# A decoder step on one core: norm weight folded into the weights' splits, set-up beside the norm, written engine order

## The chip, the core and the metric

The kernel runs on one core of one Trainium2 chip. The metric is the device time of one execution in microseconds. The kernel before took 2430.19 us (median of 3 runs, 2428.37 to 2430.72).

## The reference

One layer of a decoder trunk for 2048 prompt tokens and 8 x 4 sample tokens (2080 columns in all), float32, width 1024:

```
[u_pool | u_ssm | gates] = RMSNorm(x) * norm_mix @ w_in        # 1024 -> 512 + 512 + 2048
a     = PoolMixer(u_pool)                                      # windows of 2, 4, 8, 16 tokens
y     = S5(u_ssm)            # 32 groups, a complex diagonal scan over tokens, state 64 per group
merged = sigmoid(g0) * (a @ w_branch_pool) + sigmoid(g1) * (GLU(gelu(y)) @ w_branch_ssm)
h     = x + merged @ w_out
h     = h + SwiGLU(RMSNorm(h));   output = RMSNorm(h), and the last states of pooling and S5
```

S5 first turns its parameters into powers of a complex number: exponentials, a sine and a cosine, products (`_s5_discretise` and what follows from it).

## The kernel before, in words

Every float32 matmul is done as three float16 matmuls (`mm3`): a matrix is scaled by a power of two and split into a high half (ScalarE, ACT: `hi` = x times scale) and a low half (VectorE, DVE: `lo` = x times scale minus `hi`).

**Norm and the SSM columns** (`norm_in`). Tokens come in 16 blocks of 128 rows and one of 32. For each, ACT squares and sums (`sq`, L220), DVE makes the reciprocal root (`rstd_of`), GpSimd (POOL) multiplies the block by the norm weight (`xgp`, L230; the first two blocks on DVE, L123), the block is split (L52, L53), TensorE (PE) transposes it (L135) and ACT and DVE copy the two halves out of PSUM into `xh` and `xl` (L136). Beside that, `proj` multiplies column slices of 256 tokens with chunks 2 and 3 of `w_in`, the SSM columns; a slice has four column tiles, and ACT takes each out of PSUM (`uo`, L248), SyncE (SP) stores it to `u_d` in DRAM (L250). `w_in` is prepared by chunks of 256 columns (`Win.prep`): a sum of squares on ACT (L89), the maximum over partitions (by PE for the first chunks, by POOL for the others), a power of two by small operations on DVE (L99 to L101, L44 to L47), one split of the whole chunk.

**S5** (`S5`). `setup` loads the parameters (L391 to L422, on SP), transposes `an` and computes on DVE, about 150 operations, most of them 48 columns wide. `run` goes over four units of eight groups: matrices (`vmat`, `tmat`), states (L570), a scan on DVE (L582, L584), outputs (L643, L644). Every `yield n` of it lets `put` emit n column tiles of the other ten chunks of `w_in` (`chunk`, 100 tiles of 24 matmuls); `Win.prep` of the chunk after next stands at the start of each chunk. Then pooling, branches, output projection and the feed-forward part follow, with the remaining tiles beside the first of them.

**Order.** A planner puts each engine's instructions in order by priority (order in the program) and by what it believes to be ready. Inside `tc.manual_schedule(engines=IN_ORDER)` PE, DVE, ACT and POOL keep the written order; SP stays with the planner. Before, only the feed-forward part has it (L919). `ps` holds PSUM tiles: tag "mm" 4 banks for column tiles, "s5" 2 and "tp" 2.

Of the kernel before, what the change touches and what calls it, by code (L numbers as in the profile page):

```python
# [24 lines left out]
D = 1024  # L25
# [59 lines left out]
def pow2_root(E, x, junk, ps=None):  # L85
# [32 lines left out]
def norm_parts(E, wk, x, w, r, g, s):  # L118

    nc = E.nc  # L120
# [18 lines left out]
class Win:  # L139


    def __init__(self, E, ctx, w_in, inv_x):
        self.E, self.w, self.inv_x = E, w_in, inv_x
# [11 lines left out]
    def prep(self, c, ps=None, half=None):  # L155
# [9 lines left out]
        nc.vector.tensor_tensor(cc[:, 0:1], inv, self.inv_x, op=OP.mult)  # L165
        nc.vector.tensor_scalar(cc[:, 1:2], cc[:, 0:1], 0.5, None, op0=OP.mult)
# [13 lines left out]
def norm_in(E, ps, win, x_p, x_s, norm_mix, xh, xl, u_d):  # L180

    nc, tc = E.nc, E.tc
    with ExitStack() as ctx:
        ld = ctx.enter_context(tc.tile_pool(name="xld", bufs=7))
# [14 lines left out]
        g = bcast_row(E, wk, norm_mix, D, "gmix", bufs=1)  # L199
# [5 lines left out]
        gm = E.const.tile([128, 2], F32, name="gmx")  # L205
        nc.vector.tensor_reduce(gm[:, 0:1], g, axis=AX.X, op=OP.max, apply_absolute_value=True)
        nc.vector.tensor_scalar(gm[:, 1:2], gm[:, 0:1], 32.001, None, op0=OP.mult)
        s, inv = pow2(E, gm[:, 1:2])
        nc.vector.tensor_copy(E.inv_x, inv)
        sx = E.const.tile([128, 1], F32, name="sx")  # L210
        nc.vector.tensor_copy(sx, s)

        def norm(bs):

            w = BLK[bs[0]][1]
            steps = []
            ss = E.small.tile([128, len(bs)], F32, tag=f"ss{len(bs)}", name="ss")
            for i, b in enumerate(bs):
                sq = wk.tile([128, D], BF16, name="sq", bufs=1)
                nc.scalar.activation(sq[:w], X[b][:w], AF.Square, accum_out=ss[:w, i:i + 1])  # L220
            r = rstd_of(E, ss[:w], len(bs), w)
            rs = E.small.tile([128, len(bs)], F32, tag=f"rx{len(bs)}", name="rx")
            nc.vector.tensor_scalar(rs[:w], r, sx[:w], None, op0=OP.mult)
            for i, b in enumerate(bs):
                x = X.pop(b)
# [18 lines left out]
        def proj(n0, w, cs=((2, 0), (2, 1), (3, 0), (3, 1)), steps=()):  # L244
            for j, (c, cb) in enumerate(cs):
                q, cc = win.mm(ps, c, cb, xh, xl, n0, w)
                o = wk.tile([128, 512], F32, name="uo", bufs=3)
                nc.scalar.activation(o[:, :w], q[:, :w], AF.Copy, scale=cc[:, 0:1])  # L248
                r0 = (c - 2) * 256 + cb * 128
                nc.sync.dma_start(u_d[r0:r0 + 128, n0:n0 + w], o[:, :w])  # L250
                for f in steps[j::len(cs)]:
                    f()

        win.prep(2, ps, 0)
        for f in norm([0]):
            f()
        win.prep(2, ps, 1)
        for f in norm([1]):
            f()
        loads_to(4)  # L260
        T = {1: norm([2, 3])}
        proj(0, 128, ((2, 0), (2, 1)))
        win.prep(3, ps)
        proj(128, 128, ((2, 0), (2, 1)))
        loads_to(6)
        for p in range(7):
            if p < 6:
                T[p + 2] = norm([2 * p + 4, 2 * p + 5])
                loads_to(2 * p + 9)
            else:  # L270
                T[7] += norm([16])
            if p == 3:
                win.load(0)
            proj(p * 256, 256, ((2, 0), (2, 1), (3, 0), (3, 1))[0 if p else 2:], T.pop(p + 1))
        win.load(1)
        proj(1792, 288)
        win.prep(0)

# [19 lines left out]
NG = 32  # L298
# [11 lines left out]
def exp_f32(E, pool, x, n, tag):  # L310
# [8 lines left out]
    nc.vector.scalar_tensor_tensor(r, k, 2.12194440e-4, r, op0=OP.mult, op1=OP.add)  # L319
    nc.vector.tensor_scalar(p, r, 1.0 / 5040, None, op0=OP.mult)  # L320
    for c in (1.0 / 720, 1.0 / 120, 1.0 / 24, 1.0 / 6, 0.5, 1.0):
        nc.vector.scalar_tensor_tensor(p, p, c, r, op0=OP.add, op1=OP.mult)
    nc.vector.tensor_scalar(e.bitcast(I32), k, 127.0, 8388608.0, op0=OP.add, op1=OP.mult)
# [4 lines left out]
def sincos_f32(E, pool, x, n):  # L328
# [9 lines left out]
    tt(E, z, r, r, OP.mult)  # L338
    nc.vector.tensor_scalar(s, z, -1.9515295891e-4, 8.3321608736e-3, op0=OP.mult, op1=OP.add)
    tt(E, s, s, z, OP.mult)  # L340
    nc.vector.scalar_tensor_tensor(s, s, -1.6666654611e-1, z, op0=OP.add, op1=OP.mult)
    nc.vector.scalar_tensor_tensor(s, s, 1.0, r, op0=OP.add, op1=OP.mult)
    nc.vector.tensor_scalar(c, z, 2.443315711809948e-5, -1.388731625493765e-3, op0=OP.mult, op1=OP.add)
# [3 lines left out]
    nc.vector.tensor_scalar(c, c, 1.0, None, op0=OP.add)  # L347
    out = pool.tile([128, 2, n], F32, name="sco")
    for i, (f, o) in enumerate(((s, c), (c, s))):
# [10 lines left out]
        tt(E, out[:, i], a, sg, OP.mult)  # L360
    return out[:, 0], out[:, 1]


class S5:
# [5 lines left out]
    def setup(self):  # L370
        E, nc, w, ps = self.E, self.E.nc, self.w, self.ps
# [16 lines left out]
        with E.tc.tile_pool(name="s5s", bufs=1, side="right", reuse_waits="tile") as s:  # L388
            ld = s.tile([128, n], F32, name="ldt")
            dt = w["ssm_log_dt"]  # L390
            nc.sync.dma_start(ld[:, :NG], bass.AP(tensor=dt.tensor, offset=dt.offset, ap=[[0, 128], [1, NG]]))  # L391
            for h in range(2):
                nc.sync.dma_start(ld[h * 64:h * 64 + 64, NG:],
                                    bass.AP(tensor=dt.tensor, offset=dt.offset + h, ap=[[0, 64], [2, NG // 2]]))
            an = s.tile([NG, 2, 3, 128], F32, name="an")
            ap = ps.tile([128, 512], F32, name="mm", tag="s5", bufs=2)
            for i, nm in enumerate(("ssm_a_re", "ssm_a_im")):
                a = w[nm]
                src = a.rearrange("o g p -> (o g) p")
                nc.sync.dma_start(an[:, i, 0, 0:64], src)  # L400
                nc.sync.dma_start(an[:, i, 0, 64:128], src)
                nc.sync.dma_start(an[:16, i, 1], bass.AP(tensor=a.tensor, offset=a.offset, ap=[[128, 16], [1, 128]]))
# [4 lines left out]
            BA = s.tile([128, NG, HD], F32, name="ba")  # L407
            BB = s.tile([128, NG, HD], F32, name="bb")
            for h, (x, y) in enumerate((("ssm_b_re", "ssm_b_im"), ("ssm_b_im", "ssm_b_re"))):
                nc.sync.dma_start(BA[h * 64:h * 64 + 64], w[x].rearrange("o g p h -> p (o g) h"))  # L410
                nc.sync.dma_start(BB[h * 64:h * 64 + 64], w[y].rearrange("o g p h -> p (o g) h"))
            cn = s.tile([128, 4, 2, 128], F32, name="cn")
            for i, nm in enumerate(("ssm_c_re", "ssm_c_im")):
                src = w[nm].rearrange("o g h p -> (o g h) p").rearrange("(t r) p -> r t p", r=128)
                nc.sync.dma_start(cn[:, :, 0, i * 64:i * 64 + 64], src)
                nc.sync.dma_start(cn[:, :, 1, (1 - i) * 64:(1 - i) * 64 + 64], src)
            sn = s.tile([128, 2, 128], F32, name="sn")
            for i, nm in enumerate(("state_ssm_re", "state_ssm_im")):
                src = w[nm].rearrange("o b g p -> (o b g) p").rearrange("(t r) p -> r t p", r=128)
                nc.sync.dma_start(sn[:, :, i * 64:i * 64 + 64], src)  # L420
            nc.vector.memset(dv[96:128], 0.0)
# [1290 lines left out]
```

## Time and profile before

| | before |
|---|---|
| median of 3 runs | 2430.19 us |
| profiled execution | 2434.37 us |
| its span, first to last instruction | 2432.2 us |
| PE busy | 2298.3 us (94%) |
| DVE busy | 1641.4 us (67%) |
| ACT busy | 1021.6 us (42%) |
| POOL busy | 425.8 us (18%) |

The durations below are those of the profiled execution. In the page's slices a digit is the busy share in tenths of one fortieth of the span, 60.8 us; PEclk is the clock granted to TensorE, where 1.00 is 2.4 GHz and 0.50 is 1.2 GHz. A wait is idle time of an engine, put down to what ended it last.

### The profile page before, as it was taken

To read this page: it belongs to the slowest core of one execution; us is meant where nothing else is said; L and a number is where in the kernel's file an instruction comes from. 1 tells how busy PE (TensorE), PEld (TensorE's weight loads), DVE (VectorE), ACT (ScalarE), POOL (GpSimd) and SP (SyncE) were. 2 spreads that over 40 slices of the span, in tenths; PEclk is the share of its full clock that TensorE was granted. 3 is DMA by queue.
4 is the path that set the end of the run, shared out by engine and by line. 5 is a ranking of instruction groups with operands and counts; after the bars stand their busy time and mean duration, and the time that the engine had idled before them with its cause. 6 is when DMAs were issued, how large, how long until landed. Compare 5 with 4: busy or idle time off the path is not lost. (4 is left out here: it accounts for less than half of the span.)

```text
span 2432.2 us, 43171 instructions
## 1 busy us (share of the span) xinstructions
PE 2298.3 (94%) x16939; PEld 1613.6 (66%) x16939; DVE 1641.4 (67%) x3866; ACT 1021.6 (42%) x1808; POOL 425.8 (18%) x443
## 2 busy tenths in 40 slices
PE   5869999999999999997999999999999999989998
PEld 4745566565578875554888888888888864433543
DVE  7516784757658778777555554655555688789887
ACT  7421333323445442445444454544544552243332
POOL 2300000000000000000111221211112345355342
PEclk9889999999999999998999999999999999999999
DMA  6215133335434334413221222222212344444332
GB/s 215 72 49 124 54 90 91 102 90 198 141 118 126 114 109 159 156 64 115 70 88 53 79 76 65 79 62 79 79 53 79 126 141 142 151 169 141 122 124 78
DMA packets 209776, 258.02 MB, mean 106 GB/s; under 512 B 33046, under 2 KB 170582, under 8 KB 209053
## 3 DMA queue, kind: packets, MB, share of 16 engines
q1 hardware_dynamic: 209397, 254.83, 33.7%
q8 instruction: 132, 2.16, 0.4%
q14 instruction: 71, 0.58, 0.1%
q10 hardware_dynamic: 144, 0.26, 0.0%
q0 software_dynamic: 32, 0.18, 0.0%
HBM read 167.56 MB, written 86.67 MB: 105 GB/s over the span
## 5 line engine op out<-in xcount | busy, mean ns | idle before, releaser
L851 PEld LDWEIGHTS <-W 128*128 128x128 f16 x7392 | 726.3, 98 | 114.0 <-issue 13.9
L851 PE MATMUL p<-m,W 128*128 128x256 f16 (+1 forms) x3084 | 356.6, 275 | 1.4 <-ACT v L883 1.4
L114 PE MATMUL mm<-xl,wh 128*128 128x512 f16 (+4 forms) x1072 | 347.4, 325 | 8.0 <-DVE xl L136 8.0
L113 PE MATMUL mm<-xh,wh 128*128 128x512 f16 (+4 forms) x1072 | 347.9, 326 | 1.5 <-ACT xh L136 1.4
L115 PE MATMUL mm<-xh,wl 128*128 128x512 f16 (+4 forms) x1072 | 347.2, 325 | 1.6 <-DVE wl L53 1.6
L113 PE MATMUL pd<-m,W 128*128 128x512 f16 x616 | 236.4, 384 | 17.8 <-DVE xr L1098 7.7
L115 PE MATMUL pd<-m,W 128*128 128x512 f16 x616 | 236.3, 384 | 0.4 <-DVE W L307 0.4
L114 PE MATMUL pd<-m,W 128*128 128x512 f16 x616 | 236.6, 384 | 0.0
L851 PE MATMUL p<-x,W 128*128 128x256 f16 x1848 | 207.3, 274 | 2.9 <-ACT p L872 2.8
L851 PE MATMUL p<-xq,W 128*128 128x256 f16 x1764 | 198.4, 274 | 4.8 <-ACT p L872 3.5
L884 POOL TENSOR_TENSOR p<-v,p 128x256 f32<-128x256 f32 (+1 forms) x88 | 72.0, 818 | 666.1 <-ACT v L883 523.3
L115 PEld LDWEIGHTS <-wl 128*128 128x128 f16 x1072 | 107.1, 100 | 76.7 <-issue 9.8
L307 DVE TENSOR_TENSOR w<-u,p 128x272 f32<-128x272 f32 (+1 forms) x86 | 36.5, 425 | 172.8 <-PE p L851 169.2
L114 PEld LDWEIGHTS <-wh 128*128 128x128 f16 x1072 | 106.9, 100 | 67.5 <-issue 2.5
L113 PEld LDWEIGHTS <-wh 128*128 128x128 f16 x1072 | 106.8, 100 | 64.6 <-issue 0.3
L1097 POOL TENSOR_TENSOR xq<-xq,xr 128x512 f32<-128x512 f32 x90 | 128.8, 1451 | 42.0 <-DVE xq L1098 17.3
L114 PEld LDWEIGHTS <-W 128*128 128x128 f16 x616 | 60.9, 99 | 92.9 <-issue 23.3
L115 PEld LDWEIGHTS <-W 128*128 128x128 f16 x616 | 60.9, 99 | 75.4 <-issue 3.5
L113 PEld LDWEIGHTS <-W 128*128 128x128 f16 x616 | 60.9, 99 | 74.4 <-issue 3.4
L292 ACT ACTIVATE go<-mm,wc 128x512 f32<-128x512 f32 (+1 forms) x80 | 47.6, 603 | 139.9 <-PE mm L115 113.6
L883 ACT COPY v<-p 128x272 f32<-128x272 f32 (+1 forms) x86 | 32.2, 375 | 165.1 <-PE p L851 162.7
L113 PE MATMUL po<-woh,m 128*128 128x512 f16 x256 | 97.0, 379 | 0.9 <-DVE x L307 0.9
(472 smaller groups left out, 4429.2 us busy)
## 6 DMA issues: line engine op xcount, KB each, us to landing
f_d<-m SPq DMA_DIRECT2D x44, 512.0 KB, 3.1
xq<-f_d SPq DMA_DIRECT2D x40, 512.0 KB, 4.7
x<-in_x_prompt_dram SPq DMA_DIRECT2D x32, 512.0 KB, 4.7
xq<-h_d SPq DMA_DIRECT2D x32, 512.0 KB, 4.1
g<-g_d SPq DMA_DIRECT2D x56, 256.0 KB, 2.7
g_d<-go SPq DMA_DIRECT2D x48, 256.0 KB, 2.7
gr<-in_ffn_w_gate_dram SPq DMA_DIRECT2D x23, 512.0 KB, 4.3
ur<-in_ffn_w_up_dram SPq DMA_DIRECT2D x23, 512.0 KB, 4.9
```

Of the source, the lines that this page charges most:

```text
L113: nc.tensor.matmul(q, ah, bh, start=first, stop=False)
L114: nc.tensor.matmul(q, ah, bl, start=False, stop=False)
L115: nc.tensor.matmul(q, al, bh, start=False, stop=last)
L292: nc.scalar.activation(o[:, :w], q[:, :w], AF.Tanh, scale=cc[:, 1:2])
L307: E.nc.vector.tensor_tensor(o, a, b, op=op)
L851: nc.tensor.matmul(q, W[:, x, a, ka], X[b][:, y, k, :w], start=begin and k == v == 0, stop=end and k == 3 and v == 2, skip_group_check=True)
L883: nc.scalar.copy(v, x)
L884: nc.gpsimd.tensor_tensor(p5, v, p5, op=OP.add)
L1097: add = (lambda o, x: tt(E, o, o, x, OP.add)) if end else (lambda o, x: nc.gpsimd.tensor_tensor(o, o, x, op=OP.add))
```

## The change

The norm weight no longer multiplies the tokens; it multiplies the rows of `w_in`. The half chunks of the first chunk (2) are multiplied on DVE before their preparation; for every other chunk the split is done in eight pieces of 256 columns, each with a scale per partition that contains the weight, and the bound from the sum of squares is multiplied by the largest weight squared. POOL's product is gone. The SSM column stores are issued by ACT. S5's loads are emitted in slice 1 of the norm, and its set-up, now a generator, goes on by two pieces after each column tile from slice 3 on. Norm and S5 part stand in written order, and chunk 0 is prepared at the norm's end. The outputs of S5 are preceded by 3, 3, 5, 6 column tiles in the four units (before 10, 4, 3, 3).

```diff
-def pow2_root(E, x, junk, ps=None):
+def pow2_root(E, x, junk, ps=None, f=None):
     nc.scalar.activation(junk, x, AF.Square, accum_out=m[:, 0:1])
+    if f is not None:
+        nc.vector.tensor_tensor(m[:, 0:1], m[:, 0:1], f, op=OP.mult)
...
+SX = 512.0
-def norm_parts(E, wk, x, w, r, g, s):
-    if g is not None:
-        xg = wk.tile([128, D], F32, name="xg", tag="xg", bufs=1)
-        nc.vector.scalar_tensor_tensor(xg[:w], x[:w], r, g[:w], op0=OP.mult, op1=OP.mult)
-        x, r = xg, s[:w]
+def norm_parts(E, wk, x, w, r):
...
-    def __init__(self, E, ctx, w_in, inv_x):
+    def __init__(self, E, ctx, w_in, g):
+        self.g = E.const.tile([128, KB], F32, name="gmix")
+        E.nc.scalar.dma_start(self.g, g.rearrange("o (k p) -> p (o k)", p=128))
+        self.g2 = E.const.tile([128, 2], F32, name="gmx2")
+        E.nc.vector.tensor_reduce(self.g2[:, 0:1], self.g, axis=AX.X, op=OP.max, apply_absolute_value=True)
+        E.nc.vector.tensor_tensor(self.g2[:, 1:2], self.g2[:, 0:1], self.g2[:, 0:1], op=OP.mult)
...
-        s, inv = pow2_root(E, t[:, :, n], wh[:, :, n].bitcast(BF16), ps)
-        split(E, wh[:, :, n], wl[:, :, n], t[:, :, n], s)
+        if half is not None:
+            nc.vector.tensor_tensor(t[:, :, n], t[:, :, n],
+                                    self.g[:, :, None].to_broadcast([128, KB, n.stop - n.start]), op=OP.mult)
+        s, inv = pow2_root(E, t[:, :, n], wh[:, :, n].bitcast(BF16), ps, self.g2[:, 1:2] if half is None else None)
+        if half is not None:
+            split(E, wh[:, :, n], wl[:, :, n], t[:, :, n], s)
+        else:
+            gs = E.small.tile([128, KB], F32, tag="gs", name="gs")
+            nc.vector.tensor_scalar(gs, self.g, s, None, op0=OP.mult)
+            for k in range(KB):
+                split(E, wh[:, k], wl[:, k], t[:, k], gs[:, k:k + 1])
...
-        ld = ctx.enter_context(tc.tile_pool(name="xld", bufs=7))
+        ld = ctx.enter_context(tc.tile_pool(name="xld", bufs=6))
...
-                if b < 2:
-                    hi, lo = norm_parts(E, wk, x, w, r[:, i:i + 1], g, sx)
-                else:
-                    xg = wk.tile([128, D], F32, name="xgp", bufs=2)
-                    nc.gpsimd.tensor_tensor(xg[:w], x[:w], g[:w], op=OP.mult)
-                    hi, lo = norm_parts(E, wk, xg, w, rs[:w, i:i + 1], None, None)
+                hi, lo = norm_parts(E, wk, X.pop(b), w, rs[:w, i:i + 1])
...
+        def cols(n0, w, c, cb):
+            q, cc = win.mm(ps, c, cb, xh, xl, n0, w)
+            o = wk.tile([128, 288], F32, name="uo", bufs=4)
+            nc.scalar.activation(o[:, :w], q[:, :w], AF.Copy, scale=cc[:, 0:1])
+            r0 = (c - 2) * 256 + cb * 128
+            nc.scalar.dma_start(u_d[r0:r0 + 128, n0:n0 + w], o[:, :w])
+
+        setup = s5.setup()
+        g = norm([0])
+        step(g, 2)
         win.prep(2, ps, 0)
+        step(g)
+        put(0)
+        g = norm([1])
+        step(g, 2)
         win.prep(2, ps, 1)
+        step(g)
+        loads_to(5)
+        cols(0, 128, 2, 0)
+        put(1)
+        g = norm([2, 3])
+        step(g, 2)
+        cols(0, 128, 2, 1)
+        step(g, 2)
         win.prep(3, ps)
+        cols(128, 128, 2, 0)
+        cols(128, 128, 2, 1)
+        put(2)
+        put(3)
+        for p in range(8):
+            bs = [2 * p + 4, 2 * p + 5] if p < 6 else [16] if p == 6 else []
+            nb = [b for b in (2 * p + 2, 2 * p + 3) if p and b < 16] + ([16] if p == 7 else [])
+            g = norm(bs) if bs else iter(())
+            loads_to(2 * p + 9)
+            if p == 1:
+                s5.loads()
             if p == 3:
                 win.load(0)
+            if p == 6:
+                win.load(1)
+            f = [f for b in nb for f in T.pop(b)] if p else []
+            cc = ((2, 0), (2, 1), (3, 0), (3, 1))
+            n0, w = (p * 256, 256)
+            if p == 7:
+                for x in f:
+                    x()
+                w = 288
+            step(g)
+            for j, (c, cb) in enumerate(cc):
+                if p == 0 and j < 2:
+                    step(g)
+                    continue
+                cols(n0, w, c, cb)
+                if p < 7:
+                    for x in (f[:1], f[1:3], f[3:], ())[j]:
+                        x()
+                step(g)
+                if p > 2:
+                    step(setup, 2)
+            step(g, 4)
         win.prep(0)
+        for _ in setup:
+            pass
...
-        yield (10, 4, 3, 3)[un]
+        yield (3, 3, 5, 6)[un]
...
-        norm_in(E, ps, win, w["x_prompt"], w["x_sample"], w["norm_mix"], xh, xl, u_d)
         with ExitStack() as cs:
             s5 = S5(E, cs, ps, w, u_d, y_d, [(outs[3], outs[6]), (outs[4], outs[7])])
-            s5.setup()
+            with E.tc.manual_schedule(engines=IN_ORDER):
+                norm_in(E, ps, win, w["x_prompt"], w["x_sample"], xh, xl, u_d, s5)
+            s5.pools()
...
-            for n in s5.run():
-                put(1 if n is None else n)
+            with E.tc.manual_schedule(engines=IN_ORDER):
+                for n in s5.run():
+                    put(1 if n is None else n)
```

In the new `norm_in`, `norm(bs)` is a generator (squares; reciprocal root; one split per block), `put(b)` transposes a block and copies it out, `step(g, n)` takes n pieces of a generator. `S5.loads` holds the set-up's tiles and DMAs, `S5.setup` its 27 pieces of arithmetic with the same operations as before.

## Rows read from the trace of the kernel before

**Rows 1.** The page's slices, busy tenths in 40 slices of 60.8 us.

```profile
PE   5869999999999999997999999999999999989998
...
PEclk9889999999999999998999999999999999999999
```

**Rows 2.** Busy time by stretch: length, engines' busy us, PEclk, DMA share, GB/s.

```profile
60.00:100.00 40.00, 29.96 (x264) 25.41 (x265) 28.07 (x51) 20.83 (x29) 20.35 (x9) 0.83 0.29 93
100.00:160.00 60.00, 59.70 (x540) 47.74 (x538) 16.76 (x32) 25.20 (x33) 6.30 (x9) 1.00 0.19 61
160.00:182.00 22.00, 1.35 (x6) 0.48 (x5) 0.79 (x5) 0.69 (x1) 0.00 (x0) 0.60 0.12 9
182.00:240.00 58.00, 54.52 (x290) 30.84 (x289) 38.79 (x169) 10.07 (x15) 1.31 (x2) 0.91 0.55 126
240.00:300.00 60.00, 54.16 (x276) 32.30 (x275) 47.70 (x201) 19.93 (x37) 2.68 (x2) 0.91 0.14 48
300.00:400.00 100.00, 99.71 (x553) 60.35 (x552) 63.57 (x231) 32.23 (x64) 2.47 (x9) 1.00 0.40 95
```

**Rows 3.** PE's waits, 0 to 160 us: total, times, longest us.

```profile
PE tp L135 <- ACT hi L52: 9.2, 3, 4.6
```

**Rows 4.** ACT's groups, 0 to 160 us: count, busy us, mean ns, idle.

```profile
L220 ACT ACTIVATE sq<-x 128x1024 bf16<-128x1024 f32 x16 | 16.8, 1052 | 2.7 <-DMA x<-in_x_prompt_dram 2.6
L136 ACT COPY xh<-tp 128x1024 f16<-128x1024 f16 x16 | 16.0, 1010 | 3.6 <-PE tp L135 3.5
L52 ACT ACTIVATE hi<-xgp,rx 128x1024 f16<-128x1024 f32 x14 | 16.0, 1147 | 9.3 <-POOL xgp L230 9.3
L248 ACT ACTIVATE uo<-mm,wc 128x256 f32<-128x256 f32 x26 | 12.2, 470 | 33.1 <-PE mm L115 28.2 <-ACT hi L52 3.0 <-issue 1.8
```

**Rows 5.** PE's waits, 160 to 640 us.

```profile
PE mm L403 <- DMA an<-in_ssm_a_re_dram: 20.7, 1, 20.7
```

**Rows 6.** SP's queue, 157 to 189 us: start, us, instruction, count.

```profile
157.47 1.46 SPq L393 DMA_DIRECT2D ldt<-in_ssm_log_dt_dram  x2
...
171.57 0.60 SPq L410 DMA_DIRECT2D ba<-in_ssm_b_re_dram  x1
...
187.68 0.47 SPq L420 DMA_DIRECT2D sn<-in_state_ssm_im_dram  x1
```

**Rows 7.** DVE's groups by shape, 0 to 160 us.

```profile
L53 DVE SCALAR_TENSOR_TENSOR lo<-xgp,rx,hi 128x1024 f16<-128x1024 f32 x14 | 23.9, 1719 | 4.5 <-ACT hi L52 4.3
L136 DVE COPY xl<-tp 128x1024 f16<-128x1024 f16 x16 | 10.9, 687 | 36.8 <-PE tp L135 36.7
...
L53 DVE SCALAR_TENSOR_TENSOR wl<-wr,pw,wh 128x1024 f16<-128x1024 f32 x2 | 2.6, 1280 | 0.0
```

**Rows 8.** One source line: ACT's only DMA issue, ns min/median/max.

```profile
L1137 ACTq DMA_DIRECT2D out_dram<-xq x1: 374/374/374, 2429.3 to 2429.3; - x1
```

**Rows 9.** DVE in order of time, a chain of set-up.

```profile
182.48 1.43 DVE L322 SCALAR_TENSOR_TENSOR exa<-exa 128x48 f32<-128x48 f32 x6
```

**Rows 10.** Busy time in set-up and in one scan.

```profile
186.00:210.00 24.00, 22.20 (x130) 12.74 (x129) 23.43 (x135) 3.17 (x6) 0.00 (x0) 1.00 0.45 129
479.00:511.00 32.00, 32.00 (x172) 16.65 (x171) 32.00 (x161) 6.62 (x10) 0.35 (x1) 1.00 0.14 52
```

**Rows 11.** ACT in order of time, preparation of chunk 0.

```profile
144.06 1.91 ACT L89 ACTIVATE wh<-wr 128x2048 bf16<-128x2048 f32 x1 [2.14 <-PE mm L114]
145.88 0.19 ACT L89 ACTIVATION_READ_ACCUMULATOR wh<-wr 128x1 f32 x1
...
148.00 2.00 ACT L52 ACTIVATE wh<-wr,pw 128x2048 f16<-128x2048 f32 x1 [0.45 <-DVE wc L165]
```

**Rows 12.** ACT's groups by shape, 182 to 705 us.

```profile
L292 ACT ACTIVATE go<-mm,wc 128x512 f32<-128x512 f32 x48 | 32.6, 682 | 100.3 <-PE mm L115 82.6 <-issue 17.6
...
L519 ACT COPY v<-mm 128x512 f32<-128x512 f32 x8 | 4.4, 587 | 13.8 <-PE mm L518 13.8
...
L52 ACT ACTIVATE bh<-bt,bk 128x256 f16<-128x256 f32 x4 | 2.0, 508 | 2.0 <-DVE bt L1403 2.0
```

More of the change, by code (lines that the diff above doesn't have):

```diff
@@ L242, in loads_to, with put @@
                 nl[0] += 1
[L244 to L252, printed above, removed]
+        def put(b):
+            for f in T.pop(b):
+                f()
@@ new lines, in step @@
+        def step(g, n=1):
+            for _ in range(n):
+                next(g, None)
+        def cols(n0, w, c, cb):
[7 more added lines that the diff above has]
+        step(g, 2)
@@ L368, in __init__, with loads @@
         self.E, self.ctx, self.ps, self.w, self.u_d, self.y_d, self.outs = E, ctx, ps, w, u_d, y_d, outs
-    def setup(self):
-        E, nc, w, ps = self.E, self.E.nc, self.w, self.ps
+    def loads(self):
+        E, nc, w = self.E, self.E.nc, self.w
         K = self.ctx.enter_context(E.tc.tile_pool(name="s5k", bufs=1, side="right", reuse_waits="tile"))
@@ L387, in setup @@
         self.ymx = K.tile([128, 4], F32, name="ymx")
[L388 to L395, printed above, removed]
-            ap = ps.tile([128, 512], F32, name="mm", tag="s5", bufs=2)
[L397 to L402, printed above, removed]
+        self.lx = ExitStack()
@@ new lines, in loads @@
+        s = self.lx.enter_context(E.tc.tile_pool(name="s5l", bufs=1, side="right", reuse_waits="tile"))
+        ld = s.tile([128, n], F32, name="ldt")
+        dt = w["ssm_log_dt"]
+        nc.sync.dma_start(ld[:, :NG], bass.AP(tensor=dt.tensor, offset=dt.offset, ap=[[0, 128], [1, NG]]))
+        for h in range(2):
+            nc.sync.dma_start(ld[h * 64:h * 64 + 64, NG:],
+                              bass.AP(tensor=dt.tensor, offset=dt.offset + h, ap=[[0, 64], [2, NG // 2]]))
+        an = s.tile([NG, 2, 3, 128], F32, name="an")
@@ new lines, in loads @@
+        for i, nm in enumerate(("ssm_a_re", "ssm_a_im")):
+            a = w[nm]
+            src = a.rearrange("o g p -> (o g) p")
+            nc.sync.dma_start(an[:, i, 0, 0:64], src)
+            nc.sync.dma_start(an[:, i, 0, 64:128], src)
+            nc.sync.dma_start(an[:16, i, 1], bass.AP(tensor=a.tensor, offset=a.offset, ap=[[128, 16], [1, 128]]))
+        BA = s.tile([128, NG, HD], F32, name="ba")
+        BB = s.tile([128, NG, HD], F32, name="bb")
+        for h, (x, y) in enumerate((("ssm_b_re", "ssm_b_im"), ("ssm_b_im", "ssm_b_re"))):
+            nc.sync.dma_start(BA[h * 64:h * 64 + 64], w[x].rearrange("o g p h -> p (o g) h"))
+            nc.sync.dma_start(BB[h * 64:h * 64 + 64], w[y].rearrange("o g p h -> p (o g) h"))
@@ new lines, in loads @@
+        cn = s.tile([128, 4, 2, 128], F32, name="cn")
+        for i, nm in enumerate(("ssm_c_re", "ssm_c_im")):
+            src = w[nm].rearrange("o g h p -> (o g h) p").rearrange("(t r) p -> r t p", r=128)
+            nc.sync.dma_start(cn[:, :, 0, i * 64:i * 64 + 64], src)
+            nc.sync.dma_start(cn[:, :, 1, (1 - i) * 64:(1 - i) * 64 + 64], src)
+        sn = s.tile([128, 2, 128], F32, name="sn")
+        for i, nm in enumerate(("state_ssm_re", "state_ssm_im")):
+            src = w[nm].rearrange("o b g p -> (o b g) p").rearrange("(t r) p -> r t p", r=128)
+            nc.sync.dma_start(sn[:, :, i * 64:i * 64 + 64], src)
@@ new lines, in loads, with setup @@
+        nc.vector.memset(dv[96:128], 0.0)
+        nc.sync.dma_start(dv[112:128], w["ssm_d"].rearrange("o (g h) -> h (o g)", h=HD))
+        self.L = ld, an, BA, BB, cn, sn
+    def setup(self):
+        E, nc, w, ps = self.E, self.E.nc, self.w, self.ps
+        n = NG + NG // 2
+        P, EL, S0, S0P, BT, CT, PV = self.P, self.EL, self.S0, self.S0P, self.BT, self.CT, self.PV
+        ld, an, BA, BB, cn, sn = self.L
+        with self.lx, E.tc.tile_pool(name="s5s", bufs=1, side="right", reuse_waits="tile") as s:
+            ap = ps.tile([128, 512], F32, name="mm", tag="s5", bufs=2)
+            for i in range(2):
@@ L406, in setup @@
             nc.vector.tensor_copy(A.rearrange("p a n -> p (a n)"), ap[:, :2 * n])
[L407 to L421, printed above, removed]
-            nc.sync.dma_start(dv[112:128], w["ssm_d"].rearrange("o (g h) -> h (o g)", h=HD))
-            dte = exp_f32(E, s, ld, n, "exa")
+            yield
+            dte = yield from exp_f32(E, s, ld, n, "exa")
             ang = s.tile([128, 2, n], F32, name="ang")
@@ L428, in setup @@
             tt(E, ang[:, 1], A[:, 1], dte, OP.mult)
-            mag = exp_f32(E, s, ang[:, 0], n, "exb")
-            si, co = sincos_f32(E, s, ang[:, 1], n)
+            mag = yield from exp_f32(E, s, ang[:, 0], n, "exb")
+            si, co = yield from sincos_f32(E, s, ang[:, 1], n)
             nc.vector.memset(P[:, 0, 0], 1.0)
@@ L1575, in trunk @@
     nc.scalar.activation(warm[:, 2:3], warm[:, 0:1], AF.Tanh)
-    for nm in ("inv_x", "ymax", "amax"):
+    for nm in ("ymax", "amax"):
         setattr(E, nm, E.const.tile([128, 1], F32, name=nm))
```

68 lines of the change are left out of this document (30 added, 38 removed).

## The prediction

> **What bounds the kernel now.** I read the page's slices first. PE is at 9 tenths or more in nearly every slice; the exceptions that matter here lie at the front, slices 1 to 3 and the fifth, where one digit of PEclk also dips to 8 [rows 1]. So this is a kernel bound by TensorE: a microsecond taken out of PE's queue at the front moves everything behind it forward, and one hidden beside PE is worth nothing. Second view: busy time by stretch. Between 60 and 100 us PE works 29.96 of 40 us at a mean clock of 0.83; between 160 and 182 us it works 1.35 of 22 us; then 54.5 of 58 and 54.2 of 60 us, both at 0.91; from 300 us on it is full (99.7 of 100, clock 1.00) [rows 2]. Third, the waits of PE: in the norm the largest is on `hi`, 9.2 us [rows 3], and `hi` itself waited for POOL's product with the norm weight [rows 4]; after it there is one single wait of 20.7 us, for the DMA of `an` [rows 5]. Why that DMA is late is seen in SP's own queue: it issues the two strided loads of `ldt` at 157.5 us, `ba` only at 171.6, and the last of S5's set-up loads at 187.7 [rows 6]. The set-up's DMAs thus take 31 us of a queue, and they start when the norm ends, so that PE soon has nothing beside them.
>
> **What the change takes away.** (a) Loads and set-up arithmetic move beside the norm, so the wait for `an` goes: 20.7 us. (b) POOL's product goes. PE's idle time between 60 and 100 us is 40 - 29.96 = 10.0 us; the clock of 0.83 means that 34% of the stretch, 13.6 us, stood at 1.2 GHz, of which at least 3.6 us were busy. I count 10 + 3 = 13 us. VectorE also gets its own time back: `lo` takes 1.72 us on average while POOL runs, where the same shape without POOL takes 1.28 [rows 7]. (c) From 182 to 300 us PE idles 3.5 + 5.8 = 9.3 us, and 18% of 118 us, 21.2 us, stands at 1.2 GHz; half of that, 10.6 us, is lost if PE was busy in all of it. Together 19.9, of which I count 19. Sum: 53 us.
>
> **What it adds.**
> *Start.* In written order three things stand on the first path that the planner had put elsewhere: two products of a half chunk of weights with the norm weight (128x1024, 1.28 us each by the nearest row [rows 7]), the square of block 1 behind the copy of block 0 (1.0 us), and chunk 3's preparation behind the splits of blocks 2 and 3 (1.15 + 1.28 us). 2.6 + 1.0 + 2.4 = 6 us. Against it stands VectorE without POOL; so -4 to +10. The norm weight's own load is now 1024 pieces of 4 bytes on ACT's queue; I let it land before it is needed (about 8 us), else it costs up to 4 of the 10.
>
> *ACT in the norm.* The stores of the SSM columns cost ACT an issue each, 0.374 us by the only DMA that ACT issues [rows 8]. A slice (256 tokens: four column tiles on PE) then has on ACT 2 x 1.05 + 2 x 1.15 + 2 x 1.01 + 4 x (0.47 + 0.37) = 9.8 us [rows 4, 8]. On PE it has 4 x 24 matmuls of 256 columns, 10.2 us at 2.4 GHz, and 32 transposes of 128 columns, 1.7: 12 us. ACT is covered by 2 us a slice; without that cover each slice would be ACT's.
>
> *Set-up on VectorE.* A slice has there 2 x 1.28 (`lo`), 2 x 0.69 (`xl`) and 13 small operations of 0.2 [rows 9], 2.6: in all 6.5 us [rows 7]. The set-up began with one chain of 15 operations of 0.2 [rows 9], 3.0 us, and then filled 23.4 us of VectorE in the planner's order, which runs two or three chains side by side: 135 operations in 23.43 us, 0.17 each [rows 10]. Written as one chain it goes at 0.24 (six in 1.43 us [rows 9]); with about 115 small ones that is 0.07 x 115 = 8 more, 34 us. It is put, two pieces per column tile, into slices 3 to 6, which have 4 x 12 = 48 us on PE; VectorE would hold 26 + 34 = 60 of it, or 52 at the planner's rate. The copy of `xl` that the next slice's matmuls need stands behind four pieces in each slice, and slice 4 holds 11 of the 34 us. PE therefore waits between 5 and 15 us, most at the end of slice 4; 0 if the chains overlap as before and slack takes the rest. I take 8.
>
> *Entry into the S5 part.* Chunk 0 is now prepared behind the last projection: on ACT the eviction 0.47 and its issue 0.37, the square 1.91 + 0.1, 1.93 us to the first split (145.88 + 0.19 to 148.00 [rows 11]), 0.3 for two new small operations, first piece 0.51 [rows 12]: 5.6 us in which PE has nothing. Then PE has two tiles of 24 x 512 columns, 10.2 us, and 1.0 of transposes, so it is done 16.8 us after the norm's end. Its next step needs a PSUM bank that ACT's copy of V frees, and on ACT that copy stands behind chunk 0's other pieces (to 9.2), chunk 1 (2.0 + 2.2 + 8 x 0.508 = 8.3), chunk 4 (8.3; its load waits for chunk 0's raw buffer and has 8 us to land), two evictions (1.4) and itself (0.59): 27.8 us [rows 12]. Wait: 11 us; 7 if the squares overlap VectorE's part, 13 if chunk 1's small operations stand behind the three products of `vt`. This is where most of the removed wait comes back.
> [...]
>
> *Units of S5.* A scan fills VectorE for 32.0 us (479 to 511 us, fully busy [rows 10]); four copies of the state 2.8 (0.69 each, the size of `xl` [rows 7]), and 1.2 preparations per unit inside it, each 8 pieces of 0.5 and 1.9 of small operations [rows 11, 12], 5.9. In unit 1 the scan can start after three tiles and V's step, 16 us after the states: 16 + 32 + 2.8 + 7.1 = 58 us against 13 tiles of 4.16 (24 x 416 columns on average at 2.4 GHz) and some 2.7 for V's step, 56.8, on PE; unit 2, which has one tile less before the scan and one less in all, 53.4 against 52.6. So PE waits 2 us, and 3 more where VectorE stands at a preparation until PE's tile is evicted: 5, between 0 and 16. Three tiles fewer run beside S5 (65 for 68) and three more beside the pooling part: no change while PE is full there.
>
> *Clock.* Every wait of this list can be followed by a stretch at 1.2 GHz, as those of [rows 2] are; before, 10.6 + 3 us were lost to it with 40 us of idle time. With 30 us of waits, partly short: 5, between 0 and 10.
>
> Added: 6 + 8 + 5.6 + 11 + 5 + 5 = 40.6. Net 53 - 40.6 = 12.4 us less. The profiled execution took 2434.37 us (span 2432.2); it becomes 2422.0, and since the median of the timed runs, 2430.19, lies 4.2 lower: 2418 us.
>
> **Rivals.**
> R1, everything hides: set-up in VectorE's idle time, units covered, only the entry gap (5.6), a shorter wait for V (7) and 1 of clock remain: 53 - 13.6 = 39 less, 2391. For it: VectorE is at 17 of 60 us between 100 and 160 us [rows 2]. Against: the order within a slice, not the sum, decides.
> R2, slower: VectorE's written queue in slices 3 to 6. If the one chain with its semaphores takes 45 us for 34, VectorE holds 71 us of slices that PE could do in 48; after slack PE waits 20 (12 more than taken), with two more stretches at 1.2 GHz (7 more): -12.4 + 19 = +6.6, 2437. It decides from about 42 us of set-up on. For it: no second chain is left to fill the gaps. Against: adjacent products are still independent.
> R3, no change: S5's loads hold SP's queue for 31 us as in [rows 6], now in front of blocks 12 to 15. Begun once blocks 10 and 11 have their buffers, near 60 us, they let block 12 land at about 96, and slice 4 wants it at 93. If other traffic stretches them by 10 us more, PE waits that long: 2428. SP is not in the written order, so the planner can also place them earlier, which costs nothing.
>
> **How the numbers follow.** Forecast 0.44 (its own range 2408 to 2425), R1 and what lies towards it 0.25, R3 and others near zero 0.14, R2 and other ways to slower 0.17. From no change, a measurement here can tell 0.2%, 4.9 us: faster 0.69, same 0.14, slower 0.17. The bounds added up give 46 us less to 23 more; for 8 in 10 I take 2388 to 2438.
>
> **What would show it.** The wait for `an` is absent and S5's loads are issued before 100 us. Right: PE idles 5 to 6 us before chunk 0's first matmul and near 11 us before the first L522, for ACT's copy of V (L519); VectorE is full in slices 3 to 5 and PE waits there for `xl`. Wrong: no wait at V (R1), waits for `xl` of 15 us and more (R2), ACT's squares waiting for `x` loads (R3). A norm that ends before 140 us would mean that my set-up term is too large; one after 160 that the start is worse than 10.

## The result, and the profile after

The changed kernel takes 2456.45 us (median of 4 runs, 2454.67 to 2459.78) beside 2429.96 for the kernel before on the same chip: a ratio of 1.011 (95% interval 1.009 to 1.013), so 26 us slower, where 12 us less were forecast. Its profiled execution has a span of 2458.0 us. One execution of e10 below (5099 us, the profiled one, so that no rows of that run are read) and one of e14 (4637 us) were far longer than the others, and the ratios leave them out.

The page's slices after the change; in [rows 1] the same two lines begin 5869 and 9889:

```profile
PE   3889999899999999998999999999999999988998
...
PEclk8989989999999999999899999999999999999999
```

The first slice has fallen from 5 to 3, slices 2, 3 and 8 are at 8, and the clock shows an 8 in slices 1, 3 and 6 (before, in slices 2 and 3). By stretch (columns as in [rows 2]):

```profile
0.00:60.00 60.00, 19.96 (x176) 17.58 (x177) 27.20 (x92) 24.39 (x38) 2.39 (x11) 0.83 0.63 170
60.00:100.00 40.00, 38.87 (x399) 35.10 (x398) 21.14 (x77) 28.34 (x42) 0.00 (x0) 1.00 0.46 143
100.00:160.00 60.00, 48.17 (x457) 41.65 (x455) 51.96 (x202) 25.41 (x37) 0.29 (x2) 0.91 0.12 36
160.00:182.00 22.00, 16.07 (x102) 10.19 (x101) 6.51 (x30) 10.38 (x19) 0.71 (x2) 0.84 0.40 80
182.00:240.00 58.00, 52.74 (x282) 31.86 (x280) 37.96 (x144) 22.41 (x48) 1.60 (x4) 0.91 0.40 110
240.00:300.00 60.00, 57.33 (x305) 33.44 (x304) 31.83 (x107) 22.49 (x48) 1.65 (x5) 1.00 0.32 81
300.00:400.00 100.00, 93.66 (x484) 54.36 (x482) 62.86 (x244) 31.51 (x68) 2.00 (x6) 0.93 0.35 87
```

Against [rows 2] the gains are there: 38.9 of 40 us for 30.0 between 60 and 100 us, 16.1 for 1.35 between 160 and 182. They are given back in three places: at the front (19.96 of 60 us at a clock of 0.83; the kernel before has 34.44 at 0.97 there, below), between 100 and 160 us (48.2 for 59.7, with VectorE now at 52 for 17), and in the S5 part from 300 us on (93.7 at 0.93 for 99.7 at 1.00). Between 182 and 300 us less came back than was counted: PE still stands 5.3 + 2.7 us (9.3 before), and its clock stays at 0.91 up to 240 us. The first stretch of the kernel before:

```profile
0.00:60.00 60.00, 34.44 (x346) 30.07 (x346) 46.78 (x163) 42.90 (x61) 16.86 (x17) 0.97 0.64 214
```

PE's waits after the change, from 0 to 160 us and from 160 to 640 us (total, times, longest); the wait for `an` [rows 5] is gone, and that on `hi` [rows 3] is halved:

```profile
PE mm L97 <- DVE pr L91: 17.4, 1, 17.4
...
PE mm L116 <- DVE xl L136: 8.6, 4, 5.7
...
PE tp L135 <- ACT hi L52: 4.7, 2, 3.7
```

```profile
PE mm L115 <- ACT go L331: 10.4, 1, 10.4
PE mm L592 <- ACT v L589: 8.5, 4, 4.8
PE mm L115 <- ACT wh L52: 5.9, 1, 5.9
```

The largest one first. PE waits for the scale of chunk 3's weights; VectorE and ACT are behind ACT's first store. SP's queue (with `...` for the lines between) and then ACT in order of time:

```profile
17.79 1.47 SPq L440 DMA_DIRECT2D ldt<-in_ssm_log_dt_dram  x2
19.30 4.99 SPq L446 DMA_DIRECT2D an<-in_ssm_a_re_dram  x1
...
31.22 0.60 SPq L452 DMA_DIRECT2D ba<-in_ssm_b_re_dram  x1
40.12 0.60 SPq L453 DMA_DIRECT2D bb<-in_ssm_b_im_dram  x1
```

```profile
28.24 0.34 ACT L257 ACTIVATE uo<-mm,wc 128x128 f32<-128x128 f32 x1
40.36 0.36 ACTq L259 DMA_DIRECT2D u_d<-uo  x1
40.77 1.01 ACT L136 COPY xh<-tp 128x1024 f16<-128x1024 f16 x1 [12.18 <-DMA an<-in_ssm_a_re_dram]
```

The two strided loads of `ldt` (1024 pieces of 4 bytes each), which held SP's queue in [rows 6], now run at 18 us, in the middle of the start, and ACT's store, on another queue, goes out only when `bb` does, 12 us after its data was ready. In the kernel before the hold was longer than [rows 6] shows: between `ba` at 171.57 and the last load stands

```profile
180.85 0.60 SPq L411 DMA_DIRECT2D bb<-in_ssm_b_im_dram  x1
```

so `bb` came 23 us after the first of the strided loads there, and 22 us after the change. In ten of these microseconds (22 to 32 us after the change) the record of single DMA packets has

```profile
DMA packets 1079, 0.00 MB, mean 0 GB/s; under 512 B 1079, under 2 KB 1079, under 8 KB 1079
```

and they keep the 16 DMA engines busy for 4.7% of the time: the small pieces come at some 108 a microsecond, and nearly nothing else moves. The second place, the S5 run: ACT, and then VectorE, around the wait of 10.4 us:

```profile
438.85 3.30 ACT L52 ACTIVATE wh<-wr,gs 128x256 f16<-128x256 f32 x8 [22.36 <-DVE gs L175]
442.06 0.67 ACT L331 ACTIVATE go<-mm,wc 128x512 f32<-128x512 f32 x1
```

```profile
435.96 0.61 DVE L654 SCALAR_TENSOR_TENSOR r<-r,el,r 128x127 f32<-128x127 f32 x2
436.49 0.15 DVE L91 TENSOR_TENSOR pr<-pr,gmx 128x1 f32<-128x1 f32 x1
...
438.52 0.23 DVE L175 TENSOR_SCALAR gs<-gmix,pw 128x8 f32<-128x8 f32 x1
```

ACT stands 22.4 us in front of the pieces of a chunk, because their scale `gs` is queued on VectorE behind the scan. PE's finished tiles wait for eviction behind those pieces (the 10.4 us end at 442.77).

### The profile page after: what moved, and what is told of

The parts are those of the page before. It is cut to its first block, busy times and chain, and to the rows that moved or that the text cites. A ratio compares the mean times of both kernels' runs of the same rounds, so it can differ in the third digit from the quotient of the medians.

```text
span 2458.0 us, 43291 instructions
## 1 busy us (share of the span) xinstructions
PE 2299.6 (94%) x16939; PEld 1614.1 (66%) x16939; DVE 1642.5 (67%) x3959; ACT 1036.8 (42%) x1885; POOL 383.3 (16%) x428
## 5 line engine op out<-in xcount | busy, mean ns | idle before, releaser
L115 PE MATMUL mm<-xh,wh 128*128 128x512 f16 (+4 forms) x1072 | 352.2, 329 | 17.2 <-ACT go L331 10.4
L116 PEld LDWEIGHTS <-wh 128*128 128x128 f16 x1072 | 107.9, 101 | 78.8 <-issue 14.3
```

The costliest lines, as they stand in the source:

```text
L115: nc.tensor.matmul(q, ah, bh, start=first, stop=False)
L116: nc.tensor.matmul(q, ah, bl, start=False, stop=False)
```

## The experiments

Each was timed in alternation with the kernel before; medians, and the ratio to before with its interval. S is the changed kernel, "planned" means that the planner orders the engines, "written" that the order of the text holds.

**1. The start and the two written orders.**

```diff
 e1_ldt: S with
-            nc.sync.dma_start(ld[h*64:h*64+64, NG:], <dt, offset h, step 2>)
+            nc.vector.tensor_copy(ld[h*64:h*64+64, NG:], ld[h*64:h*64+64, h:NG:2])
 e2_s5plan: S with
-            with E.tc.manual_schedule(engines=IN_ORDER):
-                for n in s5.run(): ...
+            for n in s5.run(): ...
 e3_both: both edits
 e4_uosp: S with
-            nc.scalar.dma_start(u_d[r0:r0 + 128, n0:n0 + w], o[:, :w])
+            nc.sync.dma_start(u_d[r0:r0 + 128, n0:n0 + w], o[:, :w])
```

e1_ldt. 

> One edit to the changed kernel: the two strided loads of ldt (1024 pieces of 4 bytes each) are replaced by two VectorE copies from the part already loaded; all else as changed. Theory S (start): in the changed kernel ACT stands 12.2 us (28.2 to 40.4 us) at its first store of u_d, and PE then 17.4 us before chunk 3's scale, because descriptors of these 2048 small pieces are ahead; without them the store issues at once and the wait falls to 5 us or less: 12 to 16 us less than the changed kernel, 2441 to 2445, and still slower than before. Theory V (the S5 part makes all of the loss, the start is paid back later by set-up waits): 2452 to 2457. Both leave the losses after 300 us as they are.

e2_s5plan. 

> One edit to the changed kernel: the S5 run is no longer in written order, the planner orders it; norm part as changed. Theory W (the written order of the S5 run costs): PE loses 42 us between 300 and 600 us after and 14 before; so 24 to 30 us less, 2426 to 2433. Rival U (the new yields 3,3,5,6 and the chunk preparations in eight pieces cost, not the order): within 6 us of the changed kernel, 2450 to 2459.

e3_both. 

> Both edits (ldt copied on chip, S5 run in the planner's order). If the start and the S5 run are two separate losses they add: 2456 less 13 less 27, 2416 (2410 to 2420), faster than before by 10 to 20. If the start's gain is swallowed by VectorE's set-up in slices 3 to 6, within 4 us of the kernel with only the S5 run in the planner's order.

e4_uosp. 

> One edit to the changed kernel: the stores of the SSM columns go back from ACT's queue to SP's. Theory S (ACT itself is held by the store that it issues): PE's wait of 17.4 us at chunk 3's scale falls below 7, 10 to 13 us less, 2443 to 2446. Rival (the small pieces hold all transfers, and blocks or chunk 3's weights come late whatever issues the store): the wait stays over 12 us and the time within 5 us of the changed kernel.

Measured: e1 2445.56 (1.006, 1.0045 to 1.0075), 10.9 less than S; e2 2456.21 (1.0108), nothing; e3 2444.85 (1.0056); e4 2455.95 (1.0101), nothing. In e1 the store goes out at once (ACT in order of time) and PE has 29.13 us in the first 60 for 19.96:

```profile
28.75 0.35 ACT L257 ACTIVATE uo<-mm,wc 128x128 f32<-128x128 f32 x1
29.12 0.34 ACTq L259 DMA_DIRECT2D u_d<-uo  x1
```

So the small pieces cost 11 us here, a little under what theory S said (12 to 16). e4 shows that ACT's stall is not the price by itself: with the stores on SP the wait at chunk 3 falls to 6.5 us, but then SP's own transfers are late (the store goes out at 41.03 us and the next load of `x` at 44.25, in S at 41.99) and PE waits 7.5 us for `lo` (PE's waits of e4, 0 to 160 us):

```profile
PE tp L135 <- DVE lo L53: 8.6, 3, 7.5
...
PE mm L97 <- DVE pr L91: 6.5, 1, 6.5
```

e2 and e3 refuted theory W in this form: with the S5 run planned, PE works 50.0 of the 50 us between 400 and 450 us in e3, 39.6 in S, but a new wait takes the place of that loss, for `st`, the scan's states that the products of the outputs need (PE's waits of e3, 160 to 640 us):

```profile
PE mm L713 <- DVE st L707: 24.2, 2, 23.0
```

**2. The yields, the preparations, the norm's order, and the loads in the kernel before.**

```diff
 e5_planyield: e3_both with
-        yield (3, 3, 5, 6)[un]
+        yield (10, 4, 3, 3)[un]
 e6_staged: e1_ldt; a chunk's preparation as a generator, one stage per column tile
-                    if i + 2 < len(order):
-                        win.prep(order[i + 2])
+                    a = ahead(i)          # square / reduce / scale / 2 pieces at a time
+                    for _ in chunk(...):
+                        next(a, None)
 e7_before_ldt: the kernel before with the edit of e1_ldt
 e8_noorder: e5_planyield with
-            with E.tc.manual_schedule(engines=IN_ORDER):
-                norm_in(...)
+            norm_in(...)
```

e5_planyield. 

> The kernel with ldt copied on chip and the S5 run in the planner's order, and now the old number of chunk tiles in front of the outputs, (10, 4, 3, 3) for (3, 3, 5, 6). Theory Y: PE's single wait of 23.0 us for st (241.4 us) in that kernel is there because only 3 tiles stand between scan 0 and its outputs; with 10 it goes, 2444.9 less 20 to 24: 2421 to 2425, faster than before. Rival: VectorE's scan of unit 0 is late for another reason (set-up, chunk preparations) and PE runs out somewhere else: within 8 us of 2445.

e6_staged. 

> The changed kernel with ldt copied on chip, S5 run in written order as changed; only the chunk preparations are given out in stages, one stage for each column tile (square; scale; two pieces at a time), where the changed kernel writes each whole in one place. Theory P (ACT and VectorE each stand in the middle of a preparation until the other has done its tile or its piece of the scan: ACT 22.4 us at 438 us, VectorE 29.7 us at longest for a square): PE's losses between 300 and 450 us (22 us) fall to 8 or less and the wait for V goes: 2445.6 less 14 to 22, 2424 to 2432. Rival Q (the scan with the yields 3,3,5,6 fills VectorE whatever the preparations do): 2440 to 2446.

e7_before_ldt. 

> The kernel before with one edit: the two strided loads of ldt replaced by two VectorE copies. The 20.7 us wait for an: theory S says 14 of them are the 2048 small pieces that hold SP's queue from 157.5 to 171.6 us, so 10 to 15 less than before: 2416 to 2421. Rival: the set-up's arithmetic on VectorE (23 us) and the other loads are as long behind, PE then waits for those: 2425 to 2431.

e8_noorder. 

> As the kernel with ldt copied, planner's order and old yields in the S5 run, and now the norm with its set-up also in the planner's order: of the change only the folded norm weight, the stores on ACT's queue and the earlier set-up are left. If the written order in the norm costs (set-up between the tiles, a preparation at the entry: about 16 us lost between 100 and 180 us), 5 to 15 us less than the kernel with the written norm; if it pays, 3 to 10 us more.

Measured: e5 2433.87 (1.0013, 1.0003 to 1.0022), e6 2449.17 (1.0076), e7 2403.95 (0.9888, 0.9872 to 0.9905), e8 2391.33 (0.9836, 0.9821 to 0.9851). e5 fell between its theories: the old yields are worth 11 us, but the wait for `st` stays (23.1 us). It stays, at 22.6 to 25.6 us, in every kernel here with a written norm and a planned S5 run, and is 1.2 us at most in e8; why the planner puts PE's step so early after a written block was not settled. e6 was a miss: ACT's wait for `gs` is halved (10.4 us at the longest), and its copies of `y` come late instead (PE's waits of e6, 160 to 640 us):

```profile
PE mm L741 <- ACT y L743: 16.1, 4, 8.8
```

e7 shows that the strided loads alone made the wait for `an`: with two copies of 0.17 us in their place it is 1.1 us. With 26.5 us less in all it is also a miss: 10 to 15 were expected, from a hold of 14 us that was 23. And e8 is the surprise, 42.5 us under e5 where 5 to 15 were expected: without the written orders, with the loads mended and the old yields, the change is 39 us faster than before. e5 and then e8 by stretch:

```profile
0.00:60.00 60.00, 29.29 (x296) 25.74 (x297) 32.30 (x110) 32.28 (x49) 2.39 (x11) 0.91 0.72 200
...
100.00:180.00 80.00, 66.09 (x524) 49.84 (x522) 57.12 (x207) 33.98 (x57) 2.21 (x8) 0.91 0.26 72
180.00:300.00 120.00, 95.65 (x516) 54.59 (x514) 58.00 (x248) 35.35 (x71) 2.02 (x4) 0.89 0.23 66
```

```profile
0.00:60.00 60.00, 42.81 (x456) 37.49 (x457) 42.52 (x177) 49.53 (x76) 2.39 (x11) 1.00 0.83 239
...
100.00:180.00 80.00, 77.34 (x548) 52.09 (x546) 42.27 (x116) 33.22 (x68) 2.36 (x8) 1.00 0.43 104
180.00:300.00 120.00, 104.71 (x582) 61.74 (x580) 74.49 (x312) 35.25 (x73) 3.02 (x7) 0.93 0.30 81
```

PE gets 13.5 us more in the first 60, 11.3 more between 100 and 180, at a granted clock of 1.00 for 0.91, and 9.1 more between 180 and 300. In that last stretch e5 has the wait for `st`; e8 has another in its place, at an eviction (PE's waits of e8, 160 to 640 us):

```profile
PE mm L115 <- ACT go L328: 15.1, 1, 15.1
```

**3. One written part at a time.**

```diff
 e9_normplan: e1_ldt with the norm planned (the edit of e8), the S5 run written, (3, 3, 5, 6)
 e10_strided: e8_noorder with the strided loads of ldt back
 e11_thin: e5_planyield with
-                if p > 2:
-                    step(setup, 2)
+                if p > 0:
+                    step(setup)
 e12_noorder_staged: e8_noorder with the staged preparations of e6
```

e9_normplan. 

> The changed kernel with ldt copied on chip; norm and set-up in the planner's order, the S5 run in written order as changed (3, 3, 5, 6). Theory N (the norm's written order makes the loss: 30 us of the lost PE time by 200 us, 68.7 against 39.1): 2445.6 less 25 to 35, 2411 to 2421, and still 15 to 25 slower than with both parts planned. Rival N0 (the written S5 run costs nothing beside the planned one, as with the written norm, where 2445.6 and 2444.9 were measured): 2391 to 2403.

e10_strided. 

> The change with both parts in the planner's order and the old yields, but the two strided loads of ldt as before (2048 pieces of 4 bytes). Theory S: the pieces hold queue and ACT's store as in the changed kernel, whatever the order: 2391.3 plus 9 to 13, 2400 to 2404. Rival: the planner has other work in front while the transfers wait: 2390 to 2395.

e11_thin. 

> Norm in written order, S5 run planned with the old yields, ldt copied (2433.9); now the set-up is given out one step a tile from slice 1 on, where it had two steps a tile from slice 3 on. Theory G (the set-up's steps clump and hold back xl: 5.7 us in slice 4, and ct 3.5, and the half clock after them): 5 to 10 less, 2424 to 2429. Rival (VectorE's sum, or another wait, sets the norm's end): 2431 to 2437.

e12_noorder_staged. 

> Both parts in the planner's order with the old yields and ldt copied (2391.3); now the chunk preparations are emitted in stages. Theory P2 (at 188 to 216 us ACT waits 27.2 us for gs, which stands behind the scan on VectorE, and PE 15.1 us for the eviction behind it; staged, gs is asked for earlier): the 15.1 us go, 2376 to 2383. Rival (the planner orders by its own estimate, the order of emission changes little): 2388 to 2396.

Measured: e9 2408.9 (0.9913, 0.9898 to 0.9928), e10 2403.43 (0.9889), e11 2426.02 (0.9982), e12 2390.7 (0.9838). The norm's written order costs 36.7 us (e1 to e9; in neither is the wait for `st` over 1.7 us), the small pieces 12 in a planned order too (e8 to e10), and the clumps of set-up 7.9 (e5 to e11): N (a little over its range), S and G hold. PE's time rises from e1 to e9 by 14.3 us in the first 60 (29.13 to 43.44) and by as much between 100 and 180 (61.65 to 75.82). With the norm planned, the written S5 run and its yields together cost 17.6 (e9 to e8), which N0 denied; no run has the written S5 run with the old yields, so the two are not told apart, and with the norm written, planning the S5 run alone gave nothing (e2, e3). In e12 the staging moved nothing: the wait for the eviction is 13.9 us there and 15.1 in e8.

**4. Inside the norm's order.**

```diff
 e13_nodve: e5_planyield, norm_in under
+            with E.tc.manual_schedule(engines=IN_ORDER - {mybir.EngineType.DVE}):
 e14_onlydve: e5_planyield, norm_in under
+            with E.tc.manual_schedule(engines={mybir.EngineType.DVE}):
 e15_start: e11_thin; both products and squares of chunk 2, then chunk 3's square,
   ahead of the splits of blocks 1 to 3
 e16_entry: e15_start; chunk 0's preparation staged, from slice 5 on
-        win.prep(0)
+                if p > 4:
+                    step(first)
```

e13_nodve. 

> Norm in written order on PE, ACT and POOL, VectorE's order left to the planner; S5 run planned with the old yields, ldt copied (2433.9 with VectorE written too, 2391.3 with all planned). Theory D (VectorE's written queue with the set-up in it makes most of the 42 us): 2405 to 2418. Theory A (the order of the first preparations on ACT: chunk 3's square starts at 48.7 us in the changed kernel, at 16.0 us where all is planned): 2424 to 2433, PE's wait of 7.3 us at chunk 3's scale stays.

e14_onlydve. 

> The reverse: only VectorE in written order in the norm, PE, ACT and POOL planned. Theory D: 2424 to 2434. Theory A: 2400 to 2412.

e15_start. 

> Norm in written order on all engines with the thin set-up (2426.0); the first preparations now stand as the planner puts them: both products, both halves' squares, then chunk 3's square ahead of blocks 1 to 3's splits. PE lost 39.4 us up to 60 us with the written start and 23.9 where all is planned. If the start is a loss of its own: 12 to 16 less, 2410 to 2414. If VectorE gives it back in the slices after it: 2420 to 2426.

e16_entry. 

> As the kernel with the mended start, and chunk 0's preparation given out in stages in slices 5 to 7 instead of standing whole behind the last projection. The term 'entry' (PE idle 3.0 us there with the thin set-up, 2.8 before it for vt, and a half clock behind them): 4 to 8 less than the kernel with the mended start. Rival: VectorE is full in these slices, and xl comes later for it: 0 to 4 more.

Measured: e13 2414.35 (0.9934, 0.9918 to 0.9951), 19.5 less than e5; e14 2429.1 (0.9994, 0.9985 to 1.0004), 37.8 more than e8; e15 2417.43 (0.9945), 8.6 less than e11; e16 2419.68 (0.9953), 2.3 more than e15. Both runs of the first pair fall as theory D said. But the parts don't add: with VectorE's order alone 38 of the 42.5 us are lost, with the other engines' alone 23. Part of that is counted in both. Each still has the wait for `st`, where e8 has the 15.1 us for an eviction (PE's waits of e13, then of e14, 160 to 640 us):

```profile
PE mm L713 <- DVE st L707: 25.5, 2, 24.3
```

```profile
PE mm L713 <- DVE st L707: 26.7, 2, 25.5
```

And each has 34 us of PE time in the first 60 (34.05 and 34.28) where e8 has 42.81. So neither number is the price of one engine's queue by itself. The mended start gave less than it should (8.6 of 12 to 16), and moving chunk 0's preparation only moved the wait: its rival holds (`xl` 4.9 us at 129 us in place of the entry).

**5. The lock of ACT and VectorE in the S5 part.**

```diff
 e17_early: e8_noorder, prep(c) in two, the scale a chunk earlier
-                        win.prep(order[i + 2])
+                        win.cut(order[i + 2])
+                        if j == 3 and i + 3 < len(order):
+                            win.stat(order[i + 3])
 e18_const: e9_normplan, prep(c) for chunks 1 and 4 to 11
-        s, inv = pow2_root(...)
+        s, inv = self.S1        # chunk 0's
```

e17_early. 

> Both parts in the planner's order, old yields, ldt copied (2391.3); the square and the scale of a chunk's weights are now taken a chunk earlier than its pieces, so that ACT no longer waits for gs behind the scan. If the 15.1 us at 204 us are this lock: 2376 to 2382. If the planner puts the scale behind the scan again or another wait takes its place: 2387 to 2395.

e18_const. 

> Norm planned, S5 run in written order with 3, 3, 5, 6, ldt copied (2408.9); chunks 1 and 4 to 11 take chunk 0's scale, so their squares, reductions and scales are left out. If the preparations' lock of ACT and VectorE makes the written S5 run's loss (14.5 us between 340 and 400 us, 10.7 of it one wait for the eviction): 2390 to 2398. If the order of the scan, its copies and the yields makes it: 2403 to 2409.

Measured: e17 2394.09 (0.9852), e18 2391.35 (0.9841, 0.9826 to 0.9855). e18 takes away 17.5 of the 17.6 us of the written S5 run, so the time hangs on the preparations' squares, reductions and scales. But the lock that it was built to remove is still there: `gs` is made from the constant by VectorE, still behind the scan, and ACT waits for it nearly as long as in e9 (22.15 us for 22.65), PE 8.3 us for 10.7 (ACT of e18 in order of time):

```profile
375.31 3.30 ACT L52 ACTIVATE wh<-wr,gs 128x256 f16<-128x256 f32 x8 [22.15 <-DVE gs L183]
```

PE has 9.4 us more work between 200 and 500 us than in e9 (286.0 for 276.6), and which of the things left out gave them is open; e8 with the same constants, which might gain too, was not run. Nor does the lock belong to the written order: e8, planned, has the longer wait of 15.1 us. e17, which also has one buffer fewer for the SSM column tiles (3 for 4), is a miss that names the next lock: the square now stands on ACT ahead of its load (PE's wait is 19.5 us; ACT in order of time):

```profile
195.23 0.69 ACT L348 ACTIVATE go<-mm,wc 128x512 f32<-128x512 f32 x1 [1.51 <-issue]
227.94 1.91 ACT L89 ACTIVATE junk<-wr 128x2048 bf16<-128x2048 f32 x1 [32.02 <-DMA wr<-in_w_in_dram]
```

e8 and e12, at 2391, beat both kernels by 39 and 65 us.

## Why the prediction was wrong, point by point

*What the change takes away* (53 us) was right in kind for (a) and (b). The wait for `an` went, and the stretch from 60 to 100 us got 8.9 us of PE time and its full clock. (c) was taken too large: 19 us were counted between 182 and 300, where idle time and slow clock, 19.9 us by the prediction's reckoning, are still 5.3 + 2.7 + 5.2 = 13.2 after the change, 4.8 of them the wait for V that is a term of its own. With both orders planned and the old yields, strided loads and all, the change is 27 us faster than before (e10); R1's figure of 2391 is e8's to the microsecond, but only with the loads mended as well, so that is coincidence and not R1's sum come true.

*Start* (6, between -4 and +10) is the step that failed first. PE has 14.5 us less in the first 60 than before, and at a lower clock. Two causes: the small pieces (10.9, e1), and the order of the first preparations (8.6 come back in e15, in another kernel, so the two need not add). The first is my clause in R3, that the planner "can also place them earlier, which costs nothing". I priced the move of S5's loads against blocks 12 to 15, near 60 us, but SP is not in the written order, and the planner put them at 17 us. The queue had the price: 14 us for `ldt` in [rows 6], 23 with the line above. I read it as part of a wait that goes away, where it was a cost that moves with the loads. The norm weight's own load was no part of it: issued at 0.73 us, it was read at 5.17. The prediction's own test, that a norm which ends after 160 us shows a worse start, came out so: the last stores of the norm are issued at 170.9 us.

*Set-up on VectorE* (8, between 5 and 15) was right in size and place: 8.6 us of waits for `xl`, 5.7 of them at the end of slice 4, and 7.9 back in e11. What was missed is that the written order costs beyond the set-up. Start and set-up together were 14; the norm's order costs 36.7 on top of the loads (e1 to e9). R2 named VectorE's queue as the place and 19 us as the price; e13 gives 19.5 for releasing that queue. Whether R2's condition (42 us of set-up) held was not measured; R2's 19 were 12 of waits and 7 of clock, so that the two numbers agree proves little.

*Entry into S5*: 5.6 forecast, 5.9 measured. The wait for V was 4.8, not 11: PE came to that step 2.6 us later than forecast, the first ten matmuls of its tiles at a granted clock of 0.50 (176.3 to 180.5 us; 0.84 on the mean from 160 to 182), and V's copy ended 3.6 us earlier. About 2.3 of these are the pieces: I took 0.508 us for each from [rows 12], and the eight pieces above run in 3.30, so 0.41 each, with records of 0.495 us on the mean. The row's mean is the length of one record, and these records overlap where pieces follow each other.

*Units of S5* (5, between 0 and 16) was mis-sized as well: 17.6 for the written run with its yields (e9 to e8), which go when the preparations' squares and scales are left out (e18), though the longest wait stays. I had counted VectorE's time and a 3 us stand "until PE's tile is evicted". The real wait runs the other way: ACT waits for VectorE's scan, 22.4 us at the longest, and PE for ACT.

*Clock* (5) has no run of its own. With PE's waits the clock fell too: 0.91 in e5 between 100 and 180 us, 1.00 in e8. No record gives the clock in GHz. What the forecast calls 1.2 and 2.4 GHz are two levels that the trace of the kernel before shows after the wait for `an`: matmuls of 512 columns start 0.43 us apart where the granted clock is 0.50 (183 to 184 us) and 0.215 us apart where it is 1.00 (from 186 us on), about 1.2 and 2.4 columns a nanosecond.

*Range*. The terms' own bounds add up to 44 us less (the set-up at 0) and 17 more, not to 46 and 23; the 26 measured lie beyond both. And the first reading names a fifth slice that [rows 1] does not show: only slices 1 to 3 are below 9 there.

The sum by the runs: the planned change with mended loads -39.1 (e8), the written S5 run +17.6 (e9), the written norm +36.7 (e1), the small pieces +10.9 (S): 26.1 of the 26.5 us. Each step is the difference of two neighbouring runs, so the sum has to close, and the sizes hold in this order of steps only: the S5 run's 17.6, order and yields together, were 11.7 with the norm written (e1 to e5), 11.0 of them the yields (e3 to e5).

## What to carry to other kernels

When loads are moved, the slow pieces in them move too: look up in the queue's rows what each costs, and ask whom they will now hold up; here a strided load of 4-byte pieces was better made on chip from one that is there (two copies of 0.17 us; 10.9 us less in e1, 26.5 in e7). An order written for one engine is a set of waits for all of them (with VectorE's alone written in the norm, e14 takes 37.8 us more than e8): before it is written, follow each short chain that hops between engines (square, scale, pieces, eviction) and see what long work stands in front of its middle link. And try the parts of such a change without the order first; here they were worth 27 to 39 us (e10, e8), and the order cost more than that.

## What the runs showed of the hardware

2048 pieces of 4 bytes, 8 KB in all, took from 18 to 40 us (issued at 17.79, with `bb` behind them at 40.12; in e8, without them, `bb` goes out at 25.67), with the DMA engines 4.7% busy from 22 to 32, and ACT's store on its own queue was held for 11.8 of these. Without the pieces the same store was issued 0.02 us after its data was ready (e1). Their size alone does not make the price: the norm weight's 1024 pieces of 4 bytes, on ACT's queue, were there 4.4 us after their issue. That loads on one queue hold an issue on another was not expected; by what means, the descriptors of theory S or something else, no run here tells.
